# The two transposes that turn an expert's inner layer are issued in the middle of the next expert's first product

## The chip, the cores and the metric

The kernel runs on one core of a Trainium2 chip. The metric is device time in microseconds (us) of one execution. The engines are named as the profile names them: PE is TensorE, DVE VectorE, ACT ScalarE, POOL GpSimd, and SP issues transfers. Every engine works off its own instructions in the order in which they were built.

## The reference, cut to what matters

One layer of a hybrid decoder is computed for 512 prompt and 8 sample tokens (520 rows of 1024): a projection, dilated attention, a state space branch, a merge, a layer norm, and then a mixture of experts with 64 experts, of which each token takes 8. All of it is float32. The part that the change touches is the body of the experts' loop:

```
xb = x_pad[tok]                                   # rows of one expert
h  = jax.nn.silu(xb @ w1[e]) * (xb @ w3[e])       # 1024 -> 256
yb = (h @ w2[e]).astype(jnp.float32)              # 256 -> 1024
return acc.at[tok].add(yb * g[:, None])
```

A shared expert, a gated side input and a second layer norm are added to the result.

## The kernel before, in words

The experts are taken in an order of falling load, and the place of an expert in it is its rank, 0 to 63. A rank has a fixed capacity of 112 down to 56 rows. Float32 products are made as three products of float32r halves: an operand is split into `hi` (a rounded copy, by ScalarE) and `lo` (what is left, by VectorE, or by GpSimd for one item of six), and hi·hi, hi·lo and lo·hi are accumulated (`split`, L267 to L270).

The weights of a rank are six items of 128x1024: four for the first product (w1 and w3 side by side) and two for the second (w2). Each is loaded into one of seven buffers `raw` (L318), split into one of five pairs `hi`, `lo`, and used. `stream.get` (L339) asks for the split of two items beyond the one that it returns.

For rank e the steps are these. `turn` (L1416) transposes the gathered rows, `a<-ident,xg`, in two halves of four transposes, and splits each half into `xgh` and `xgl`. `expert_in` (L1427) makes the first product, `a<-hi,xgh` and so on: four items of six matmuls, 24 in all, into one bank of PSUM, and `ffn_mid` (L1252) makes of it `hg`, by a Silu on ScalarE (L1254) and a product on VectorE. `ffn_turn` (L1258) turns `hg` with two transposes, `a<-ident,hg`, into another bank, and splits that into `hh` (ScalarE) and `hl` (VectorE). `expert_out` (L1435) makes the second product, `mm<-hi,hh` and so on, two items of six matmuls; ScalarE scales it into `y` and GpSimd adds its rows into DRAM by an indirect transfer (L1449). All tiles `a` come from a pool of three banks.

The loop (L1597) issues in iteration e the first product of rank e, the turning of the rows of rank e+1, the second product of rank e-1, and then the turning of `hg` of rank e. So between two first products stand a second product and transposes. Side work (the shared expert, the side input: `x<-ph,...`) is spread over the iterations. The code's order isn't the engines' order: a scheduler places the instructions of each engine by priority and by its own model of time, and takes buffers and banks as it goes. All matmuls have line L210 and all transposes L215, since they go through a helper.

Of the kernel before, what the change touches and what calls it, by code (L numbers as in the profile page):

```python
# [11 lines left out]
def _quiet(*args, **kwargs):  # L12
# [19 lines left out]
NE = 64  # L32
FIXED = 2
CAPS = ([112] * 3 + [100] * 1 + [94] * 1 + [92] * 1 + [88] * 2 + [86] * 1 + [84] * 3 + [82] * 2 + [78] * 7 + [76] * 2 + [74] * 4
        + [72] * 5 + [70] * 4 + [68] * 4 + [66] * 5 + [64] * 7 + [62] * 3 + [60] * 2 + [58] * 2 + [56] * 5)
# [165 lines left out]
def trunk_step(ctx: ExitStack, tc: tile.TileContext, I, O):  # L201
# [3 lines left out]
    class Tensor:  # L205
# [3 lines left out]
        def matmul(self, *a, **k):  # L209
            ins = nc.tensor.matmul(*a, **k)  # L210
            if self.pinned:
                tc.keep_in_program_order(ins)

        def transpose(self, *a, **k):
            ins = nc.tensor.transpose(*a, **k)  # L215
            if self.pinned:
                tc.keep_in_program_order(ins)

    T = Tensor()
# [11 lines left out]
    def open_pool(*a, **k):  # L231
        cm = pool(*a, **k)
        p = cm.__enter__()
        opened.append((p, cm))
        return p

    def close_pool(p):
        at = next(n for n, (q, _) in enumerate(opened) if q is p)
        opened.pop(at)[1].__exit__(None, None, None)
# [15 lines left out]
    def bank():  # L255
        return psa.tile([128, 512], F32, tag="a", name="a")
# [10 lines left out]
    def split(hi, lo, src, e=V):  # L267

        a = S.activation(hi, src, AF.Copy)  # L269
        return a, sub(e, lo, src, hi.bitcast(F32))  # L270
# [974 lines left out]
    def ffn_in(out, xth, xtl, hi, lo, q, rows):  # L1245

        for k in range(2):
            kk = 2 * q + k
            for n, (l, w) in enumerate(((xth, hi), (xth, lo), (xtl, hi))):
                T.matmul(out, lhsT=l[:, kk, rows], rhs=w[:, k], start=(kk == 0 and n == 0), stop=(kk == 7 and n == 2))  # L1250

    def ffn_mid(ps, m):  # L1252
        hg = moe.tile([MAX_CAP, 256], F32, tag="hg", bufs=2, name="hg")
        S.activation(hg[0:m], ps[0:m, 0:256], AF.Silu)  # L1254
        mul(V, hg[0:m], hg[0:m], ps[0:m, 256:512])
        return hg

    def ffn_turn(hg, m):  # L1258
        ps = bank()
        for k in range(2):  # L1260
            T.transpose(ps[:, m * k:m * k + m], hg[0:m, 128 * k:128 * k + 128], ident[0:m, 0:m])
        hh, hl = (moe.tile([128, 2, MAX_CAP], F32R, tag=nm, bufs=2, name=nm)[:, :, 0:m] for nm in ("hh", "hl"))
        H['turned'] = split(hh, hl, ps[:, 0:2 * m].rearrange("p (k t) -> p k t", k=2))
        return hh, hl
# [9 lines left out]
    def shared_mid(out, hg):  # L1274
        S.activation(hg, out[:, 0:128], AF.Silu)
        mul(V, hg, hg, out[:, 128:256])
        return hg

    def shared_turn(hg, i, c):

        ps = bank()
        T.transpose(ps[:, 0:TT], hg, ident[0:TT, 0:TT])
        split(H['shared'][:, i, 0, c], H['shared'][:, i, 1, c], ps[:, 0:TT])
# [12 lines left out]
    def shared_more(i):  # L1296

        if i < 0:
            side_weights(lambda a, b: wd[50 + a // 1024], 2048)
            H['ph'], H['pl'] = (H[k][:, 0:2048].rearrange("p (k n) -> p k n", k=8) for k in ('ph', 'pl'))  # L1300
            return
        out = psx.tile([128, 512], F32, tag="x", name="x")[0:TT, 0:256]
        whole(shared_product(out, i, H['ph'], H['pl'], range(8)))
        shared_turn(shared_mid(out, moe.tile([MAX_CAP, 256], F32, tag="hg", bufs=2, name="sg")[0:TT, 0:128]), i, 1)
# [67 lines left out]
    def second_sums(i):  # L1372

        G.dma_start(H['x1'][:, i], sumsD[1][TT * i:TT * i + TT], accum_op=ALU.add)


    XG, XT, HG, HT, GC, IX = {}, {}, {}, {}, {}, {}
# [28 lines left out]
    def fetch(e):  # L1406
        find(e)
        gather(e)
# [7 lines left out]
    def turn(e):  # L1416
        x, m = XG[e % 3], CAPS[e]
        XT[e] = [moe.tile([128, 8, MAX_CAP], F32R, tag=nm, bufs=2, name=nm)[:, :, 0:m] for nm in ("xgh", "xgl")]
        for z in range(2):
            ps = bank()  # L1420
            for j in range(4):
                k = 4 * z + j
                T.transpose(ps[:, m * j:m * j + m], x[0:m, 128 * k:128 * k + 128], ident[0:m, 0:m])
            src = ps[:, 0:4 * m].rearrange("p (k t) -> p k t", k=4)
            split(XT[e][0][:, 4 * z:4 * z + 4], XT[e][1][:, 4 * z:4 * z + 4], src)

    def expert_in(e):  # L1427
        ps, m = bank(), CAPS[e]
        for q in range(4):
            hi, lo = (t.rearrange("p (k n) -> p k n", k=2) for t in stream.get(AT[e] + q))  # L1430
            ffn_in(ps[0:m], *XT[e], hi, lo, q, slice(0, m))
        HG[e] = ffn_mid(ps, m)
        XT.pop(e)

    def expert_out(e):  # L1435
        ps, m = mm2(), CAPS[e]
        hh, hl = HT.pop(e)
        for k in range(2):
            hi, lo = stream.get(BT[e] + k)
            for n, (l, w) in enumerate(((hh, hi), (hh, lo), (hl, hi))):  # L1440
                for h in range(2):
                    T.matmul(ps[0:m, h], lhsT=l[:, k], rhs=w[:, 512 * h:512 * h + 512], start=(k == 0 and n == 0),
                             stop=(k == 1 and n == 2))
        if e >= NE - 2:
            kept(e, ps)
            return
        y = py.tile([MAX_CAP, 1024], F32, tag="y", bufs=YB, name="y")[0:m]
        S.activation(y.rearrange("p (h n) -> p h n", h=2), ps[0:m], AF.Copy, scale=GC.pop(e)[0:m])  # L1448
        G.indirect_dma_start(out=sumsD[e % 2 if e < SECOND else 0][:, :], out_offset=bass.IndirectOffsetOnAxis(ap=IX.pop(e)[0:m, 0:1], axis=0),  # L1449
                             in_=y, in_offset=None, compute_op=ALU.add)  # L1450
# [24 lines left out]
    def second_phase():  # L1475
# [109 lines left out]
        for e in range(3):  # L1585
            fill(F[1])
            find(e, (1,))
        T.pinned = False
        expert_in(0)
        turn(1)  # L1590
        HT[0] = ffn_turn(HG.pop(0), CAPS[0])
# [5 lines left out]
        for e in range(NE + 1):  # L1597
            if e == NE - 1:
                last_rows()
            if 0 < e < NE:  # L1600
                expert_in(e)
            if 0 < e < NE - 1:
                turn(e + 1)
            if e:
                expert_out(e - 1)
            else:
                H['shared'] = py.tile([128, 5, 2, 2, TT], F32R, tag="side", name="st")
                mids = py.tile([MAX_CAP, 1024], F32, tag="y", bufs=YB, name="mids")
                mids = [shared_mid(H['first half'][i], mids[0:TT, 128 * i:128 * i + 128]) for i in R5]
            if 0 < e < 6:  # L1610
                shared_turn(mids[e - 1], e - 1, 0)
            if 0 < e < NE - 1:
                HT[e] = ffn_turn(HG.pop(e), CAPS[e])
            if e + 3 < NE:
                fetch(e + 3)
            for i in {SECOND + 2: (0, 1, 2), SECOND + 3: (3, 4)}.get(e, ()):
                second_sums(i)
            if e == 4:
                close_pool(pre)
                pw = open_pool("pw")  # L1620
            while side and (e - 4) * SIDE >= N_SIDE - len(side) + 1:
                q, i = side.pop(0)
                if q == -2:
                    shared_more(i)
                elif q == -1:
                    shared_out(i)
                elif q < 4:
                    layer_inputs(q, i)
                else:
                    last_scales(i)  # L1630
# [66 lines left out]
    def last_rows():  # L1697

        yy = pw.tile([128, 2, 1024], F32R, tag="pl", name="yy")
        H['yh'], H['yl'] = yy[:, 0], yy[:, 1]  # L1700
        to = H['to'] = pw.tile([128, 5, TT], F32R, tag="praw", name="to")
        G.memset(yy.bitcast(F32), 0.0)
        G.memset(to.bitcast(F32), 0.0)
        for e in (NE - 2, NE - 1):
            m, z = CAPS[e], 64 * (NE - 1 - e)
            oh = OH.pop(e)
            for tiles in ((0, 1, 2), (3, 4)):
                ps = mm2()[:, 0]
                for n, i in enumerate(tiles):
                    T.matmul(ps[z:z + m, TT * n:TT * n + TT], lhsT=oh[:, i], rhs=ident_b[0:TT, 0:TT], start=True, stop=True)  # L1710
                a, b = tiles[0], tiles[-1] + 1
                S.activation(to[z:z + m, a:b], ps[z:z + m, 0:TT * len(tiles)].rearrange("p (i t) -> p i t", t=TT), AF.Copy)
# [116 lines left out]
    close_pool(gpool)  # L1829
    close_pool(qkv)  # L1830
    second_phase()


# [16 lines left out]
```

## Time and profile before

| | us |
|---|---|
| three runs | 1322.67, 1334.91, 1335.15 |
| their median | 1334.91 |
| the profiled execution | 1326.8 |
| its span, first to last instruction | 1325.1 |

The experts take the span from about 450 to 1290 us. The profile names for each idle time of an engine the instruction that ended it. A row of the timeline gives start, length, instruction, and in brackets the idle time before it with what ended it. Matmuls overlap, so the distance of two starts is the time that one costs.

### The profile page before, as it was taken

What the parts mean: (1) busy time and instruction counts of PE and PEld (TensorE: products, weight loads), DVE (VectorE), ACT (ScalarE), POOL (GpSimd) and SP (SyncE); (2) the same over time, 40 slices, a digit from 0 to 9 for tenths busy, and PEclk for the clock granted to TensorE, in tenths of its full rate; (3) what the DMA queues carried; (4) which work ended last, traced back from release to release, by engine and by line L of the source; (5) the groups of instructions that cost most, each with busy time, mean ns of one, the idle gap of its engine ahead of it and who ended that gap; (6) DMA issues with size and microseconds to landing.
All of it is one profiled execution on the core that took longest, in us unless ns stands there. A gap on an engine that the chain in (4) does not pass through costs nothing. (4 is left out here: it accounts for less than half of the span.)

```text
span 1325.1 us, 20407 instructions
## 1 busy us (share of the span) xinstructions
PE 1188.6 (90%) x7083; PEld 887.7 (67%) x7084; DVE 939.5 (71%) x1397; ACT 700.4 (53%) x1055; POOL 535.2 (40%) x327
## 2 busy tenths in 40 slices
PE   7699999999998979888899888899999999988683
PEld 7699799899877856556566566667666666644341
DVE  7974657833468778576779566788877887766566
ACT  4131535222213566566567556677767776766462
POOL 1822141011124446343656335454554544455325
PEclk9897899999997989888999889999999999989897
DMA  8476563253343699889989978999999999979973
GB/s 295 124 255 114 188 202 121 83 143 96 112 149 103 196 266 252 255 264 294 310 253 322 299 232 280 286 335 318 332 319 309 335 318 293 291 254 279 256 218 93
DMA packets 114236, 312.93 MB, mean 236 GB/s; under 512 B 37041, under 2 KB 37465, under 8 KB 113055
## 3 DMA queue, kind: packets, MB, share of 16 engines
q1 hardware_dynamic: 68307, 247.11, 54.8%
q0 software_dynamic: 30848, 43.33, 15.0%
q10 hardware_dynamic: 14974, 21.14, 6.0%
q8 instruction: 57, 0.93, 0.3%
q14 instruction: 50, 0.41, 0.1%
HBM read 276.32 MB, written 32.87 MB: 233 GB/s over the span
## 5 line engine op out<-in xcount | busy, mean ns | idle before, releaser
L265 DVE TENSOR_TENSOR lo<-raw,hi 128x1024 fp32r<-128x1024 f32 x371 | 519.1, 1410 | 197.9 <-ACT hi L269 193.2
L269 ACT ACTIVATE hi<-raw 128x1024 fp32r<-128x1024 f32 x434 | 450.4, 1055 | 259.6 <-DMA raw<-in_we_dram 107.2
L1449 POOL DMA_INDIRECT accD<-y,idx x62 | 127.4, 2054 | 283.0 <-ACT hh L269 146.9
L210 PE MATMUL a<-hi,xgh 128*64 128x512 f32 (+18 forms) x512 | 212.7, 415 | 7.0 <-ACT hi L269 4.8
L210 PE MATMUL a<-lo,xgh 128*64 128x512 f32 (+18 forms) x512 | 210.8, 412 | 5.2 <-DVE lo L265 5.0
L210 PE MATMUL a<-hi,xgl 128*64 128x512 f32 (+18 forms) x512 | 207.6, 405 | 0.0
L265 POOL TENSOR_TENSOR lo<-raw,hi 128x1024 fp32r<-128x1024 f32 x63 | 169.7, 2694 | 54.2 <-ACT hi L269 45.2
L1412 POOL DMA_INDIRECT xg<-xD,idx x64 | 114.1, 1783 | 104.6 <-DVE idx L1394 43.2
L210 PE MATMUL mm<-xh,hi 128*128 128x260 f32 (+1 forms) x576 | 120.5, 290 | 18.9 <-DVE r L259 10.5
L210 PE MATMUL mm<-xl,hi 128*128 128x260 f32 (+1 forms) x576 | 119.1, 288 | 0.7 <-DVE xl L265 0.7
L210 PE MATMUL mm<-xh,lo 128*128 128x260 f32 (+1 forms) x576 | 119.1, 288 | 0.0
L210 PEld LDWEIGHTS a<-hi,xgh 128*64 128x64 f32 (+18 forms) x512 | 75.9, 148 | 51.8 <-ACT hi L269 8.5
L210 PEld LDWEIGHTS a<-lo,xgh 128*64 128x64 f32 (+18 forms) x512 | 76.1, 149 | 45.2 <-DVE lo L265 10.4
L210 PEld LDWEIGHTS mm<-xh,hi 128*128 128x128 f32 x576 | 91.3, 193 | 19.8 <-issue 10.8
L210 PEld LDWEIGHTS a<-hi,xgl 128*64 128x64 f32 (+18 forms) x512 | 75.6, 148 | 38.4 <-issue 4.5
L210 PE MATMUL mm<-lo,hh 128*64 128x512 f32 (+18 forms) x256 | 86.2, 419 | 15.1 <-POOL lo L265 12.5
L210 PEld LDWEIGHTS mm<-xl,hi 128*128 128x128 f32 x576 | 91.0, 193 | 1.3 <-DVE xl L265 1.0
L210 PE MATMUL mm<-hi,hh 128*64 128x512 f32 (+18 forms) x256 | 85.5, 416 | 7.1 <-ACT hi L269 6.7
L210 PEld LDWEIGHTS mm<-xh,lo 128*128 128x128 f32 x576 | 91.2, 193 | 0.1
L1448 ACT ACTIVATE y<-mm,both 78x1024 f32<-78x1024 f32 (+19 forms) x62 | 68.7, 1107 | 36.1 <-PE mm L210 33.0
L210 PE MATMUL mm<-hi,hl 128*64 128x512 f32 (+18 forms) x256 | 83.6, 409 | 0.0
L215 PEld LDWEIGHTS a<-ident,xg 64*128 64x128 f32 (+18 forms) x512 | 50.9, 146 | 43.1 <-issue 16.8
(410 smaller groups left out, 1971.4 us busy)
## 6 DMA issues: line engine op xcount, KB each, us to landing
raw<-in_we_dram SPq DMA_DIRECT2D x384, 512.0 KB
raw<-in_wd_dram SPq DMA_DIRECT2D x50, 512.0 KB
accD<-zeros_b POOLq DMA_DIRECT2D x2, 2560.0 KB
praw<-in_wp_dram SPq DMA_DIRECT2D x8, 512.0 KB
base<-in_xtok_dram ACTq DMA_DIRECT2D x1, 2080.0 KB
xD<-base ACTq DMA_DIRECT2D x5, 416.0 KB
base<-accD POOLq DMA_DIRECT2D x5, 416.0 KB
acc<-accD SPq DMA_DIRECT2D x5, 416.0 KB
```

Source lines behind the costliest of these rows:

```text
L210: ins = nc.tensor.matmul(*a, **k)
L215: ins = nc.tensor.transpose(*a, **k)
L265: return e.tensor_tensor(out=o, in0=a, in1=b, op=ALU.subtract)
L269: a = S.activation(hi, src, AF.Copy)
L1412: G.indirect_dma_start(out=XG[e % 3][0:m], out_offset=None, in_=xD[:, :], in_offset=bass.IndirectOffsetOnAxis(ap=IX[e][0:m, 0:1], axis=0), ...
L1448: S.activation(y.rearrange("p (h n) -> p h n", h=2), ps[0:m], AF.Copy, scale=GC.pop(e)[0:m])
L1449: G.indirect_dma_start(out=sumsD[e % 2 if e < SECOND else 0][:, :], out_offset=bass.IndirectOffsetOnAxis(ap=IX.pop(e)[0:m, 0:1], axis=0), ...
```

## The change

The turning of `hg` of rank e-1 is taken out of the loop's end and put into `expert_in` of rank e, behind the second of the four items, for ranks 2 to 63. Its two transposes carry an edge that keeps them behind the last matmul of that item on TensorE. The helper returns the instruction for that. Nothing is added or removed: the same transposes, splits and transfers are issued. From here on the helper's transposes have line L216 in the changed kernel and `split` L268 to L271.

```
             ins = nc.tensor.matmul(*a, **k)
             if self.pinned:
                 tc.keep_in_program_order(ins)
+            return ins
...
-                T.matmul(out, lhsT=l[:, kk, rows], rhs=w[:, k], start=(kk == 0 and n == 0), stop=(kk == 7 and n == 2))
+                ins = T.matmul(out, lhsT=l[:, kk, rows], rhs=w[:, k], start=(kk == 0 and n == 0), stop=(kk == 7 and n == 2))
+        return ins
...
         for q in range(4):
             hi, lo = (t.rearrange("p (k n) -> p k n", k=2) for t in stream.get(AT[e] + q))
-            ffn_in(ps[0:m], *XT[e], hi, lo, q, slice(0, m))
+            ins = ffn_in(ps[0:m], *XT[e], hi, lo, q, slice(0, m))
+            if q == 1 and e > 1:
+                with tc.issue_after(ins.ins):
+                    HT[e - 1] = ffn_turn(HG.pop(e - 1), CAPS[e - 1])
         HG[e] = ffn_mid(ps, m)
...
-            if 0 < e < NE - 1:
-                HT[e] = ffn_turn(HG.pop(e), CAPS[e])
```

The scheduler then places much else anew. Three places show it, with the numbers of the buffers in the names.

TensorE where `hg` of rank 28 (`hg_8375`) is turned, before. `a_8479` is the first product of rank 29, whose four items are 8395, 8407, 8480 and 8492.

```order
L210 MATMUL x_8708<-what_3592,oh_8706 70x6
L215 MATMUL a_8422<-ident_69,hg_8375 128x72 x2
L210 MATMUL a_8479<-hi_8395,xgh_8378 72x512
L210 MATMUL a_8479<-lo_8396,xgh_8378 72x512
L210 MATMUL a_8479<-hi_8395,xgl_8379 72x512
```

The same in the changed kernel, where the first product of rank 29 is `a_8472` and its items are 8395, 8407, 8473 and 8485.

```order
L210 MATMUL a_8472<-hi_8395,xgl_8379 72x512
L210 MATMUL a_8472<-hi_8407,xgh_8378 72x512
L210 MATMUL a_8472<-lo_8408,xgh_8378 72x512
L210 MATMUL a_8472<-hi_8407,xgl_8379 72x512
L210 MATMUL a_8472<-hi_8407,xgh_8378 72x512
L210 MATMUL a_8472<-lo_8408,xgh_8378 72x512
L210 MATMUL a_8472<-hi_8407,xgl_8379 72x512
L216 MATMUL a_8497<-ident_69,hg_8375 128x72 x2
L210 MATMUL a_8472<-hi_8473,xgh_8378 72x512
```

The transposes have moved from ahead of the first item's matmuls to behind those of the second.

ScalarE from one `hg` to the next `hh`, before: `hg_8375` is the inner layer of rank 28, `hh_8425` its turned half, and the items 8504 and 8516 are the second product's.

```order
L269 ACTIVATE hi_8348<-raw_8184 128x1024
L269 ACTIVATE hi_8360<-raw_8196 128x1024
L269 ACTIVATE xgh_8378<-a_8380 128x4x72
L269 ACTIVATE hi_8395<-raw_8211 128x1024
L269 ACTIVATE hi_8407<-raw_8243 128x1024
L1254 ACTIVATE hg_8375<-a_8323 72x256
L269 ACTIVATE xgh_8378<-a_8387 128x4x72
L269 ACTIVATE hi_8480<-raw_8255 128x1024
L1448 ACTIVATE y_8419<-mm_8394,both_7848 72x1024
L269 ACTIVATE hi_8492<-raw_8328 128x1024
L269 ACTIVATE hh_8425<-a_8422 128x2x72
```

The same in the changed kernel, where the turned half is `hh_8500`, and 8551 is the first item of rank 30.

```order
L270 ACTIVATE hi_8407<-raw_8243 128x1024
L270 ACTIVATE xgh_8378<-a_8380 128x4x72
L1356 ACTIVATE pt_8312<-x_8281 104x256
L1256 ACTIVATE hg_8375<-a_8316 72x256
L270 ACTIVATE hi_8473<-raw_8255 128x1024
L270 ACTIVATE xgh_8378<-a_8387 128x4x72
L270 ACTIVATE hi_8485<-raw_8321 128x1024
L1453 ACTIVATE y_8419<-mm_8394,both_7841 72x1024
L270 ACTIVATE hi_8504<-raw_8333 128x1024
L270 ACTIVATE hi_8516<-raw_8352 128x1024
L270 ACTIVATE hi_8551<-raw_8367 128x1024
L270 ACTIVATE hh_8500<-a_8497 128x2x72
```

`hg` of rank 28 stands behind the same split in both, that of rank 29's second item. `hh` stood behind the split of rank 29's fourth item, and now stands behind three more, up to rank 30's first item.

TensorE at the end of rank 29's first product, before: `hh_8425` is used, and `a_8543` is the second half of the turning of rank 30's rows.

```order
L210 MATMUL a_8479<-hi_8492,xgh_8378 72x512
L210 MATMUL a_8479<-lo_8493,xgh_8378 72x512
L210 MATMUL a_8479<-hi_8492,xgl_8379 72x512
L210 MATMUL mm_8550<-hi_8504,hh_8425 72x512 x2
L215 MATMUL a_8543<-ident_69,xg0_4185 128x72 x4
```

The same in the changed kernel.

```order
L210 MATMUL a_8472<-hi_8485,xgh_8378 72x512
L210 MATMUL a_8472<-lo_8486,xgh_8378 72x512
L210 MATMUL a_8472<-hi_8485,xgl_8379 72x512
L216 MATMUL a_8543<-ident_69,xg0_4185 128x72 x4
L210 MATMUL mm_8550<-hi_8504,hh_8500 72x512 x2
L210 MATMUL mm_8550<-lo_8505,hh_8500 72x512 x2
L210 MATMUL mm_8550<-hi_8504,hl_8501 72x512 x2
```

The second product still follows the first one, and so stands 12 matmuls of the first product behind the turning of `hg` in place of 24.

## Rows read from the trace of the kernel before

**Rows 1.** The page: the span; busy us, share and instructions of each engine.

```profile
span 1325.1 us, 20407 instructions
PE 1188.6 (90%) x7083; PEld 887.7 (67%) x7084; DVE 939.5 (71%) x1397; ACT 700.4 (53%) x1055; POOL 535.2 (40%) x327
```

**Rows 2.** Stretches: busy us of PE to POOL; granted clock, DMA share, GB/s.

```profile
600.00:650.00 50.00, 43.17 (x231) 29.47 (x230) 39.26 (x51) 35.35 (x51) 20.64 (x11) 0.93 0.92 301
1050.00:1100.00 50.00, 50.00 (x286) 31.94 (x285) 42.27 (x62) 35.51 (x50) 26.61 (x15) 1.00 1.00 326
```

**Rows 3.** Waits of TensorE, 560 to 1290 us: total us, times, longest.

```profile
PE a L215 <- DVE hg L259: 21.9, 12, 3.8
PE mm L210 <- POOL lo L265: 11.8, 10, 2.9
```

**Rows 4.** Tile hg: ns min/median/max; last, idle it ended, us, times.

```profile
L1254 ACT ACTIVATE hg<-a x64: 361/379/386, 455.6 to 1284.9; 78x256 f32<-78x256 f32 x7, 64x256 f32<-64x256 f32 x7, 72x256 f32<-72x256 f32 x5, 66x256 f32<-66x256 f32 x5
L259 DVE TENSOR_TENSOR hg<-hg,a x64: 399/407/418, 456.4 to 1285.3; 78x256 f32<-78x256 f32 x7, 64x256 f32<-64x256 f32 x7, 72x256 f32<-72x256 f32 x5, 66x256 f32<-66x256 f32 x5
...
  PE a L215: 23.5, 14
```

**Rows 5.** TensorE in time, rank 28: start us, length us, instruction [idle before <-releaser].

```profile
847.63 0.34 PE L215 MATMUL a<-ident,hg 72*128 72x72 f32 x2 [3.33 <-DVE hg L259]
...
848.04 0.39 PE L210 MATMUL a<-lo,xgh 128*72 128x512 f32 x1
848.27 0.40 PE L210 MATMUL a<-hi,xgl 128*72 128x512 f32 x1
...
848.90 0.63 PE L210 MATMUL a<-lo,xgh 128*72 128x512 f32 x1
849.32 0.63 PE L210 MATMUL a<-hi,xgl 128*72 128x512 f32 x1
```

**Rows 6.** The same stretch on ScalarE, then VectorE.

```profile
844.93 1.06 ACT L269 ACTIVATE hi<-raw 128x1024 fp32r<-128x1024 f32 x1 [3.09 <-DMA raw<-in_we_dram]
845.89 0.36 ACT L1254 ACTIVATE hg<-a 72x256 f32<-72x256 f32 x1
...
846.02 1.23 DVE L265 TENSOR_TENSOR lo<-raw,hi 128x1024 fp32r<-128x1024 f32 x1 [1.65 <-ACT hi L269]
847.16 0.41 DVE L259 TENSOR_TENSOR hg<-hg,a 72x256 f32<-72x256 f32 x1
```

**Rows 7.** TensorE, then ScalarE, where rank 26 is turned.

```profile
820.43 0.35 PE L215 MATMUL a<-ident,hg 74*128 74x74 f32 x2 [3.30 <-DVE hg L259]
...
817.73 1.06 ACT L269 ACTIVATE hi<-raw 128x1024 fp32r<-128x1024 f32 x1 [3.06 <-DMA raw<-in_we_dram]
```

**Rows 8.** TensorE where ranks 8 and 11 are turned.

```profile
569.12 0.55 PE L215 MATMUL a<-ident,hg 86*128 86x86 f32 x2 [3.27 <-DVE hg L259]
...
610.87 0.54 PE L215 MATMUL a<-ident,hg 84*128 84x84 f32 x2 [3.82 <-DVE hg L259]
```

**Rows 9.** Stretches of 10 us, TensorE: busy, granted clock, DMA share, GB/s.

```profile
610.00:620.00 10.00, 9.13 (x40) 0.68 0.77 226
840.00:850.00 10.00, 6.67 (x39) 0.93 0.91 293
850.00:860.00 10.00, 9.78 (x56) 0.90 0.88 259
```

**Rows 10.** TensorE where rank 60 is turned.

```profile
1238.88 0.46 PE L215 MATMUL a<-ident,hg 56*128 56x56 f32 x2 [3.32 <-DVE hg L259]
...
1243.71 1.10 PE L210 MATMUL mm<-lo,hh 128*56 128x512 f32 x2 [2.91 <-POOL lo L265]
```

**Rows 11.** Waits of ScalarE, 560 to 1290 us.

```profile
ACT hi L269 <- DMA raw<-in_we_dram: 96.8, 73, 3.1
```

**Rows 12.** Tile hh: what writes it and hl, ns min/median/max.

```profile
L269 ACT ACTIVATE hh<-a x64: 244/278/362, 458.7 to 1287.5; 128x156 fp32r<-128x156 f32 x7, 128x128 fp32r<-128x128 f32 x7, 128x144 fp32r<-128x144 f32 x5, 128x132 fp32r<-128x132 f32 x5
L265 DVE TENSOR_TENSOR hl<-a,hh x64: 257/300/380, 459.6 to 1288.6; 128x156 fp32r<-128x156 f32 x7, 128x128 fp32r<-128x128 f32 x7, 128x144 fp32r<-128x144 f32 x5, 128x132 fp32r<-128x132 f32 x5
```

## The prediction

> **What bounds the kernel now.** I read the page first, then stretches of the experts' stage, then who waits for whom on TensorE, and then the timeline of the longest of those waits on three engines. TensorE is busy for 90% of the span [rows 1], and the stage has two faces [rows 2]: from 1050 to 1100 us it is busy without a gap at the full clock with the transfers at a share of 1.00, while from 600 to 650 us it is busy for 43.2 of 50 us, at a granted clock of 0.93, and the transfers run at 301 GB/s where the other stretch has 326. So TensorE sets the pace, and where it has gaps, there is some room in the transfers too.
>
> The largest cause of gaps is the one that the change is about: the transposes of `hg` wait for VectorE, 21.9 us in 12 waits, about twice the next cause [rows 3]; over the whole kernel it is 23.5 us in 14 waits [rows 4]. Five of the 14 are long: 3.27 and 3.82 us at ranks 8 and 11 [rows 8], 3.30 at rank 26 [rows 7], 3.33 at rank 28 [rows 5] and 3.32 at rank 60 [rows 10], 17.0 us together, so the other nine make 6.5.
>
> The reader should now see that making `hg` takes little: 0.38 us on ScalarE and 0.41 on VectorE [rows 4]. What is long is a queue. At rank 28 ScalarE stands for 3.09 us in front of a weight split, because the item hasn't landed; the Silu that makes `hg` is behind that split on ScalarE, and the product that ends it is behind the `lo` half of the same item (1.23 us) on VectorE [rows 6]. Only then do the transposes run, at 847.63. Rank 26 shows the same with 3.06 us [rows 7]. So these waits are a late transfer that reaches TensorE by way of `hg`. What the change is worth hangs on whether TensorE has other work that doesn't need the late item.
>
> **What the change removes.** The transposes now come behind two items (12 matmuls) of the next product. A matmul costs 0.23 us at full clock (848.04 to 848.27 [rows 5]), so `hg` gets 12 x 0.23 = 2.8 us more, and an item is 6 x 0.23 = 1.4 us. By the built order, in the kernel before the split that stands right ahead of `hg` on ScalarE is the next product's second item at ranks 11 and 28, and its first item at ranks 8 and 26.
> At ranks 11 and 28 the first item is ready, so TensorE works 1.4 us of it off during the wait, and the pair of transposes (0.34 us [rows 5]) goes out of the way: 1.8 us gained each, 3.6 together. Then it stands in front of the late item itself.
> At ranks 8 and 26 the late item is the very one that TensorE wants next, with its `lo`. Only the product of `hg` (0.41) and a handover are saved, 0.5 us each, 1.0 together. At rank 60 a wait of 2.91 us for another `lo` follows [rows 10], so nothing is gained.
> Of the nine short waits I take half, 3.2 us, since the trace doesn't say for each which item is next; the bounds are 0 and 6.5.
>
> A stall also costs the clock. After the wait at rank 28 matmuls go from 0.23 to 0.42 us apart (848.90 to 849.32 [rows 5]), which is the lower level, 1.2 of 2.4 GHz. The granted clock is 0.68 over the 10 us after rank 11's stall, and 0.93 and 0.90 around rank 28's [rows 9]: 3.2 and 0.7 + 1.0 us of full-speed work lost. With stalls half as long I take half of 4.9, 2.5 us; the bounds are 0 and 4.9.
> Gained: 3.6 + 1.0 + 3.2 + 2.5 = 10.3 us, between 0 and 23.5 + 4.9 = 28.4.
>
> **What the change adds.** No instruction is added, but three slacks become short.
> First, `hh` and `hl`. The second product that needs them stood 24 matmuls behind the transposes, 5.5 us, and stands 12 behind them now, 2.8 us. And by the built order `hh` now stands on ScalarE behind the split of the item two beyond the second product's first (46 of 63 ranks), where it stood mostly behind items that TensorE needs before it. That split can begin only when the buffer of the next product's second item is free, so about when the transposes run. It takes 1.06 us [rows 6], `hh` 0.28 and `hl` 0.30 [rows 12], the `lo` between them 1.23: `hh` is there some 1.5 us behind the transposes and `hl` some 3, where they are needed at 2.8 and, four matmuls on, at 3.7. The cover is the 12 matmuls, and the margin about 1 us, if the item has landed. ScalarE waited for an item 73 times between 560 and 1290 us, 96.8 us, at most 3.1 [rows 11], so 1.3 us on average. One split in six stands ahead of `hh`: 12 such events, of which I let half exceed the margin by 1 us: 6 us, and 2 for the clock.
> Second, banks. In the built kernels the first product gets the bank of the product before it at 33 of 61 ranks, before at 16. There its first matmul, not the transposes, waits for `hg`, and the wait comes back where it was: I charge 2 us, of bounds 0 and 10.
> Third, the second half of the turning of rows always takes the bank of the turned `hg` (61 of 61, before 56) and so waits for `hl`, and the split rows are used sooner. It runs within a microsecond or two of the second product's start, so the first term holds most of it; 1 us more.
> Added: 6 + 2 + 2 + 1 = 11 us.
>
> Everything else is as before: side work moves from inside the first products to between them, but is the same; splits, gathers and scatters are the same in number on ScalarE, VectorE, GpSimd and SP, and shift with TensorE.
>
> Sum: -10.3 + 11 = +0.7 on the profiled execution's 1326.8 us, 1327.5. That execution lies 8 us below the median of the runs shown and 4 above the lowest of them, so I forecast **1328 us**, and count 1322 to 1348 us (the median within 1%) as no change, about what a measurement of this kernel can tell.
>
> **The rivals.**
> *The waits end and nothing takes their place.* For it: five stalls of over 3 us, each with a slow stretch behind, and transfers that have 8% of room where the stalls are [rows 2]. Against it: a late item stands behind each of the long ones that I followed. All of the 28.4 us gives 1298; with two thirds of it, 1308.
> *The stall moves to the second product* and grows. The place is ScalarE in front of `hh`: TensorE may not begin the second product until an item two beyond is split, so where transfers set the pace, it must keep two items in hand where one or none was enough. It decides once that split is more than 1 us late at more than one rank in four. At half of the 52 ranks from 560 to 1290 us with 1 us each, and 2 us of slow clock at one in six, it costs 26 + 17 = 43, less the 10 gained: 1360. At a quarter it costs 13 + 8 - 10 = 11: 1338. I take 1347. For it: the 73 late items [rows 11]. Against it: these 73 made only 12 waits of the transposes so far [rows 3].
> *The bank.* With the same bank in turn, Silu and product of a first product lie bare ahead of the next: 0.38 + 0.41, 0.9 us with handovers, at 17 more ranks, 15 us, so 1342. Against it: a second product of 12 matmuls, 2.8 us, stands between the two, and before, too, 16 ranks had one bank in turn.
> The Trainium skill asks for what this rival is about: in Perfetto Trace Analysis, section Matmuls, independent groups should rotate through the banks, so that ScalarE and VectorE empty one while the next group runs. By that rule alone this change would be slower; no run here shows it yet.
> That the change isn't made can be left out: the built order has the transposes behind the second item.
>
> **How the numbers follow.** My forecast has a chance of 0.50, the vanishing wait 0.25, the moved stall 0.20, the bank 0.05. Faster by over 1% is the vanishing wait, 0.25; slower is the moved stall and half of the bank, 0.22; within 1% is the rest, 0.53. The range goes from 1306, which leaves out the far half of the first rival, to 1346, which leaves out the far half of the second. The forecast's own range is 1316 to 1340.
>
> **What would show it.** In the changed profile, waits of the transposes of `hg` for VectorE should fall from 23.5 to below 5 us. What replaces them should be named: first matmuls of an item waiting for `hi` or `lo` right after a stall of ScalarE for a transfer (the late item itself), second products waiting for `hh` or `hl`, or turned rows waiting for `hl`, some 6 us, and first products waiting for `hg`, some 2. If those sums stay under 5 us and the granted clock from 600 to 650 us rises from 0.93 towards 1.00, the first rival holds. If second products wait for `hh` for over 20 us, the second does. My prediction would be wrong at its root if the items landed at other times altogether because TensorE's pace is new.

## The result and the profile after

The changed kernel takes 1347.76 us (median of six runs, 1339.29 to 1354.99), the kernel before 1332.97 in the six runs beside it: the ratio is 1.0115, with an interval of 1.0084 to 1.0146. It is slower by 1.15%, some 15 us. The forecast was 1328, and the time lies 2 us above the range of 1306 to 1346.

The profiled execution of the changed kernel is its fastest one, 1339.29 us; its span is 12.4 us longer than that of before [rows 1]. First the page, then two stretches, with the columns of [rows 2].

```profile
span 1337.5 us, 20420 instructions
PE 1189.0 (89%) x7082; PEld 887.3 (66%) x7084; DVE 969.3 (72%) x1397; ACT 707.5 (53%) x1055; POOL 537.7 (40%) x327
```

```profile
600.00:650.00 50.00, 42.77 (x254) 29.96 (x252) 34.80 (x51) 34.18 (x50) 22.54 (x11) 1.00 0.96 305
1050.00:1100.00 50.00, 49.19 (x274) 30.84 (x273) 42.23 (x56) 37.78 (x51) 23.41 (x13) 1.00 0.97 314
```

TensorE's busy time is the same, so all of the loss is in gaps, the times in which TensorE stands idle. From 600 to 650 us the clock rose from 0.93 to 1.00 and the gaps stayed. What the gaps are is in the waits of TensorE, 450 to 1290 us (total us, times, longest), of the changed kernel, the largest five, and behind them one line of the kernel before.

```profile
PE a L216 <- DMA xg<-xD,idx: 27.9, 5, 7.6
PE a L216 <- DVE hl L266: 12.4, 17, 2.1
PE mm L210 <- ACT hh L270: 9.7, 8, 2.4
PE mm L210 <- POOL lo L266: 7.9, 7, 1.8
PE a L216 <- DVE sg L260: 6.9, 5, 2.5
```

```profile
PE a L215 <- DMA xg<-xD,idx: 15.8, 3, 7.9
```

The waits for `hg`, 23.5 us [rows 4], are gone but for one of 0.7. Two things stand in their place: the short cover (`hh` for second products, `hl` for turned rows that take the same bank), 22.1 us, and rows that the gathers bring too late, 27.9 us in place of 15.8. The second was in no step of the prediction. The groups of instructions on the page (busy us, mean ns, idle us before them and what ended most of it) show on which side of the gather the delay arises, first before, then after.

```profile
L1412 POOL DMA_INDIRECT xg<-xD,idx x64 | 114.1, 1783 | 104.6 <-DVE idx L1394 43.2
```

```profile
L1414 POOL DMA_INDIRECT xg<-xD,idx x64 | 126.3, 1974 | 197.7 <-DVE idx L1396 154.7
```

GpSimd sits idle for the row numbers `idx`, 43.2 us before and 154.7 after. `idx` is what the search `x<-what,oh` on TensorE finds, so the searches come later. Rank 23 shows it. Here are TensorE and GpSimd of the changed kernel (start, length, instruction, idle before).

```profile
740.05 0.32 PE L210 MATMUL x<-what,oh 104*74 104x6 bf16 x5
...
762.44 1.22 PE L216 MATMUL a<-ident,xg 74*128 74x74 f32 x8 [7.41 <-DMA xg<-xD,idx]
...
767.23 0.63 PE L210 MATMUL a<-lo,xgh 128*74 128x512 f32 x1
767.66 0.63 PE L210 MATMUL a<-hi,xgl 128*74 128x512 f32 x1
```

```profile
743.09 2.01 POOL L1414 DMA_INDIRECT xg<-xD,idx  x1 [3.63 <-DVE idx L1396]
```

And the same rank in the kernel before.

```profile
708.16 0.32 PE L210 MATMUL x<-what,oh 104*74 104x6 bf16 x5
...
744.98 1.19 PE L215 MATMUL a<-ident,xg 74*128 74x74 f32 x8
```

```profile
712.82 2.20 POOL L1412 DMA_INDIRECT xg<-xD,idx  x1 [0.18 <-PE x L210]
```

Before, the gather is issued 32 us ahead of the turning that needs its rows; after, at 743.09, and the rows are used 19.4 us later. TensorE loses 7.41 us and then works for a while at the lower level of its clock (0.43 us from matmul to matmul, a granted clock of 0.61 over the 10 us from 762.4). Over ranks 3 to 63, a turning begins 25.0 us (median) behind the end of its gather's issue before, and 19.3 after. Why: by the order on TensorE, the search stands some 27 us of TensorE work ahead of the turning before and 20 after (matmuls of 512 columns counted at 0.23 us, of 256 at 0.12, others at 0.05; medians). Searches and side work take turns in the one `x` bank in the order of the code, and the scheduler now places most of them between the first products: of the 305 matmuls of the searches, 130 stand inside a first product before and 53 after.

ScalarE waits for weight items for 68.6 us, less than the 96.8 of [rows 11].

```profile
ACT hi L270 <- DMA raw<-in_we_dram: 68.6, 44, 3.6
```

### The profile page after: what moved, and what is told of

It reads as the page before. It is cut to its first block, busy times and chain, and to the rows that moved or that the text cites. A ratio compares the mean times of both kernels' runs of the same rounds, so it can differ in the third digit from the quotient of the medians.

```text
span 1337.5 us, 20420 instructions
## 1 busy us (share of the span) xinstructions
PE 1189.0 (89%) x7082; PEld 887.3 (66%) x7084; DVE 969.3 (72%) x1397; ACT 707.5 (53%) x1055; POOL 537.7 (40%) x327
## 5 line engine op out<-in xcount | busy, mean ns | idle before, releaser
L266 DVE TENSOR_TENSOR lo<-raw,hi 128x1024 fp32r<-128x1024 f32 x371 | 546.5, 1483 | 167.3 <-ACT hi L270 166.1
L1454 POOL DMA_INDIRECT accD<-y,idx x62 | 120.8, 1948 | 224.7 <-ACT y L1453 168.6
L1414 POOL DMA_INDIRECT xg<-xD,idx x64 | 126.3, 1974 | 197.7 <-DVE idx L1396 154.7
L266 POOL TENSOR_TENSOR lo<-raw,hi 128x1024 fp32r<-128x1024 f32 x63 | 186.1, 2954 | 36.1 <-ACT hi L270 31.4
L210 PEld LDWEIGHTS mm<-xh,hi 128*128 128x128 f32 x576 | 91.7, 194 | 22.6 <-issue 13.8
L216 PEld LDWEIGHTS a<-ident,xg 64*128 64x128 f32 (+18 forms) x512 | 50.6, 147 | 83.4 <-issue 34.6
L216 PE MATMUL a<-ident,xg 64*128 64x64 f32 (+18 forms) x512 | 63.0, 245 | 46.3 <-DMA xg<-xD,idx 27.9
L210 PE MATMUL mm<-hi,hl 128*64 128x512 f32 (+18 forms) x256 | 87.5, 425 | 0.0
```

What stands on the lines that cost most here:

```text
L266: return e.tensor_tensor(out=o, in0=a, in1=b, op=ALU.subtract)
L1414: G.indirect_dma_start(out=XG[e % 3][0:m], out_offset=None, in_=xD[:, :], in_offset=bass.IndirectOffsetOnAxis(ap=IX[e][0:m, 0:1], axis=0), ...
```

## The experiments

Theory A: the short cover of `hh` and `hl` is the loss (the prediction's second rival). Theory B: the loss is the place that the scheduler gives to searches, gathers and side work. Ratios are to the kernel before, beside it on the same chip.

**hhfirst**

```
+            if q == 3 and e > 1:
+                a, b = H['turned']
+                with tc.issue_after(a.ins), tc.issue_after(b.ins):
+                    stream.split_to(AT[e] + 6)
```

> The change, and one thing more: the splits of the items that lie beyond the second product's first one are kept behind hh on ScalarE and behind hl on VectorE. In the built order hh then stands behind the split of the second product's first item (60 of 63 ranks) and no longer behind two more; the token search of the gathers stays where the change put it (23.1 us of TensorE work ahead of the turning, changed kernel 21.5, before 27.3). Theory A (the short cover of hh and hl is what costs): waits of the second product for hh fall from 10.1 to under 4 us, those of turned rows for hl from 12.4 to about 6, and the time falls from 1348 to about 1336. Theory B (the gathers are issued late, and the gathered rows with them): gather waits stay at 15 to 30 us and the time stays at 1343 or more.

1.0182 (1.0136 to 1.0227), 1355.6 us. Theory A missed: no second product waits for `hh` any more, waits for `hl` are down from 12.4 to 0.8 us, and the loss grew. B's bounds are met (21.6 us of gather waits), but B doesn't say why the time is 8 us above the changed kernel's. ScalarE now stands in front of `hh` until the transposes have run, 7.8 us in the change and 96.1 here, and its other work stands behind it (560 to 1290 us; total, times, longest).

```profile
ACT hh L270 <- PE a L216: 96.1, 42, 5.1
```

So the new place of `hh`, behind three more splits, which the prediction counted as a cost, was the better of the two.

**fetch, q2, b_late**

```
 fetch:   fetch(e + 3) written behind expert_in(e)
 q2:      -            if q == 1 and e > 1:
          +            if q == 2 and e > 1:
 b_late (of the kernel before): fetch(e + 3) written behind the side work
```

> The change, and the search and gather of rank e+3 written right behind the first product of rank e, ahead of the turning of rank e+1. In the built order the search stands 28.4 us of TensorE work ahead of the turning that needs its rows (changed kernel 21.5, before 27.3). Turned layer still 12 matmuls ahead of the second product; hh stands behind fewer splits than in the change (at 43 of 63 ranks behind none beyond the second product's first). Theory A: some half of the 22.5 us of waits for hh and hl goes with those splits, 1340 or so, and gather waits are no matter. Theory B: gather waits fall from 27.9 to under 10 us and the late transfers behind them too, 1330 to 1336.

> The change with the turning behind the third item in place of the second: hg gets 18 matmuls, hh only 6 matmuls (1.4 us at full clock, 1.8 us in the built order) ahead of the second product. In the built order the token search stands 32.8 us ahead of the turning that needs its rows, earlier than in either kernel. The two theories go opposite ways. Theory A: hh comes 1.6 to 2.0 us behind the transposes, more than its cover at most ranks, so second products wait for hh 20 to 60 us in all, and the time is 1360 or more. Theory B: gather waits under 10 us, and the time is below the changed kernel's, 1345 or less.

> The kernel before, with the turning where it was, and only the search and gather of rank e+3 written behind the side work in place of ahead of it. In the built order the search stands 17.8 us of TensorE work ahead of the turning that needs its rows (before 27.3, changed kernel 21.5). Theory A: nothing of hh and hl changes, so within 5 us of the kernel before. Theory B: gather waits rise from 15.8 to 30 us or more and the time by at least 10 us, to 1343 or more.

fetch: 1.0063 (1.0031 to 1.0094), 1336.7 us, gather waits down from 27.9 to 0.9 us, and about half of the loss gone, between what A and B asked for. q2: 1.0070 (1.0042 to 1.0098), 1340.3 us, with half the cover of the change and 26 us of waits for `hh` and `hl`, as B asked and against theory A, which asked for 1360. b_late: 1.0101 (1.0066 to 1.0136), the change's loss without the change, as B asked. One line of fetch, two of q2 and one of b_late:

```profile
PE a L216 <- DMA xg<-xD,idx: 0.9, 1, 0.9
```

```profile
PE a L216 <- DVE hl L266: 17.8, 17, 2.9
...
PE mm L210 <- ACT hh L270: 8.4, 6, 2.4
```

```profile
PE a L215 <- DMA xg<-xD,idx: 32.6, 9, 7.1
```

**held_move.** To keep the scheduler out, a table gives each engine's instructions in the order wanted, and a chain of edges that fix the issue order alone holds them there.

```
+        hold(tc, nc)
...
+            if last is not None:
...
+                tc.add_manual_dep(i, last.name, free, reason="the table's order")
+            last = i
```

> The change's move alone. A table at the end of the loop holds every engine to the order of the kernel before; only the two transposes of each hg stand behind the second item of the next first product, the halves of the rows' turning that stood ahead of that place (33 of 122) right behind them, and the scheduler places only hh and hl. Searches, gathers and side work stand where they stood before. Theory A (the short cover of hh and hl costs): hh and hl still stand 12 matmuls ahead, so most of the loss stays, 1340 or more, with 15 us or more of waits for hh and hl. Theory B (what costs is the new place that the scheduler gives to searches, gathers and side work): the loss is gone, 1336 or less, gather waits near the 15.8 us of before. If the move itself pays the 10.3 us that the prediction put on it, below 1325.

1.0180 (1.0130 to 1.0230), 1356 us: against theory B as I had put it, and within the bounds of A. But the move wasn't alone: in an order made for other places, the transposes' users stand wrong. TensorE's second halves of rows wait for `hl` more than twice as long as in the change (27.2 us), and ScalarE stands in front of `hh` for 56.8 us, where it did so for 2.9 before.

```profile
PE a L298 <- DVE hl L348: 27.2, 24, 8.6
```

```profile
ACT hh L352 <- PE a L298: 56.8, 31, 7.8
```

**b_free_hg, a_free_rows, b_free_rows, a_free_layer, a_free_all** keep the order of their kernel by such a table, and take one dependence out (a_free_all takes out two). In their traces every engine works in the order of their own kernel, and no instruction is added. No run holds an order with nothing taken out.

```
 b_free_hg:  transpose(..., hg[0:m, ...], ...)  ->  transpose(..., ident[0:m, 0:128], ...)
 *_rows:     transpose(..., x[0:m, ...], ...)   ->  the same from rank 3 on
 *_layer:    split(hh, hl, H['xh'][:, 0:2, 0:m].bitcast(F32));  lhsT=H['xh' if l is hh else 'xl'][:, k, 0:m]
```

> The kernel before in its own order on every engine, held by a table, with one dependence taken out: the transposes of hg read the constant identity in place of hg, so they never wait for it (hg is still made; the experts' result is wrong). It prices all 23.5 us of the removed waits, with nothing put in their place. By the prediction's sum the half of it that isn't behind a late item is worth 10.3 us, 1321; if the waits only go over to the late items, hi or lo, behind them, less than 4 us, 1327 to 1333, and waits for hi and lo rise by about as much; if all goes, 1303 to 1307.

> The changed kernel in its own order on every engine, held by a table, with one dependence taken out: from rank 3 on the turning of rows reads the constant identity in place of the gathered rows, so that no transpose waits for a gather. Gathers still run. Theory B in its narrow form (late gathers alone are the loss): 28 us of waits and the slow clock behind them go, time 1330 or less. Theory A: 1342 or more, since hh and hl are as they were. If side work in one block and the short cover share the loss, in between.

> The same release in the kernel before, in its own order, held by a table: the control for the release in the changed kernel. 15.8 us of gather waits are there to go. If the two kernels differ by gathers alone, both releases end at the same time within 5 us; if not, the changed kernel stays slower by what the gathers don't explain.

> The changed kernel in its own order on every engine, held by a table, with the turned layer's dependences taken out: hh and hl are made from the halves of the normed input, and the second product reads those halves in place of hh and hl, so that no second product waits for hh or hl, and no turned row for hl (the experts' result is wrong). Gathers are as they were. The release of the rows took 21.0 us off the changed kernel and 12.4 off the kernel before, so 9.8 us of the loss are left for the layer. If they are the short cover of hh and hl (22.5 us of waits), this kernel is 8 to 12 us faster than the changed one, 1336 to 1340. If they are the order of all the rest, under 4 us.

> The changed kernel in its own order, held, with both releases: rows and layer. If gathers and cover are the whole loss, it comes down to the kernel before with its rows released, 1317, to 4 us; if the order of the rest costs too, it stays above 1322.

| | ratio | interval |
|---|---|---|
| b_free_hg | 0.9994 | 0.9972 to 1.0016 |
| b_free_rows | 0.9911 | 0.9880 to 0.9941 |
| a_free_rows | 0.9967 | 0.9946 to 0.9988 |
| a_free_layer | 1.0088 | 1.0056 to 1.0120 |
| a_free_all | 0.9999 | 0.9965 to 1.0033 |

b_free_hg: the transposes' 23.5 us of waits for `hg`, taken out with nothing put in their place, are worth nothing that the interval shows, 4 us at most. What stands there instead is waits for weight items (`hi`, `lo` on either engine), 31.2 us in all before and 46.5 here, and for the side work's `sg`, 3.0 before and 9.2 here. And 5.8 us of waits still end with `hg`: instructions that don't read it wait for the bank that it is made from. These are the longest of each kind.

```profile
PE mm L327 <- POOL lo L382: 15.2, 14, 2.5
PE a L327 <- ACT hi L386: 13.3, 7, 3.8
PE a L327 <- DVE lo L382: 9.7, 17, 1.1
PE a L332 <- DVE sg L376: 9.2, 3, 4.2
...
PE a L327 <- DVE hg L376: 4.4, 4, 2.7
```

Where the transposes had their long waits, TensorE now stands in front of these, at ranks 8, 28 and 60 (start, length, instruction, idle before).

```profile
571.54 0.31 PE L332 MATMUL a<-ident,sg 104*128 104x104 f32 x1 [4.16 <-DVE sg L376]
...
847.11 0.70 PE L327 MATMUL a<-hi,xgh 128*72 128x512 f32 x1 [2.74 <-DVE hg L376]
...
1243.63 0.67 PE L327 MATMUL a<-hi,xgh 128*56 128x512 f32 x1 [3.81 <-ACT hi L386]
```

The rows: without gather waits the changed kernel gains 0.0148 (1.0115 to 0.9967), 20 us, the kernel before 0.0089, 12 us. So late gathers are 8 us of the 15, give or take 6 by the three intervals. The layer: without any wait for `hh` or `hl` the changed kernel gains 0.0027 with its gathers, give or take 0.0045, and nothing without them (0.9967 to 0.9999, give or take 0.0039). So 22 us of waits for the layer cost about nothing, and theory A falls; released of its gathers alone, the changed kernel shows even more of them and is a little faster than the kernel before.

```profile
PE mm L315 <- ACT hh L375: 18.7, 12, 4.6
PE a L321 <- DVE hl L371: 15.6, 20, 1.8
```

**a_mm, b_mm, a_mm_q0**

```
-        ps = bank()
+        if e is None:
+            ps = bank()
+        else:
+            H['mm', e] = mm2()
+            ps = H['mm', e][:, 1]
...
-            for n, (l, w) in enumerate(((hh, hi), (hh, lo), (hl, hi))):
-                for h in range(2):
+            for h in range(2):
+                for n, (l, w) in enumerate(((hh, hi), (hh, lo), (hl, hi))):
```

> The change, with the turned hg written into one half of the second product's own PSUM buffer (two of them, rotating) in place of one of the three banks; the second product is issued half by half, so that the half with the turned hg comes last. In the built order the second half of the rows' turning stands inside the first product again at 49 of 60 ranks (changed kernel 0, before 33), and the search 26 us ahead of its turning (changed kernel 20, before 27). hh and hl still stand 12 matmuls ahead of the second product. Theory D (the middle of a first product is the place where the three banks are short: the product holds one, the turned hg takes the one that the rows' turning needs, and everything behind it moves back): waits of turned rows for hl go from 12.4 to under 2 us, gather waits to 16 or less, time 1336 or less and within 5 us of the same buffer in the kernel before. Theory A (short cover of hh and hl): 10 us or more of waits for hh stay and the time is 1340 or more.

> The control: the same buffer for the turned hg in the kernel before, with the turning where it was (24 matmuls ahead). Both theories: within 1% of the kernel before, 1320 to 1340; theory D: the changed kernel with this buffer is as fast to 5 us; theory A: that one is slower by 10 us or more.

> As the change with the turned hg in the second product's buffer, and the turning behind the first item in place of the second: 18 matmuls of cover for hh in place of 12 (4.9 us in the built order in place of 3.5, control 6.1). Theory A: its time lies between that of the control and that of the change with this buffer, some 4 us under the latter. Theory D: no difference among the three beyond 5 us.

a_mm 1.0103 (1.0070 to 1.0136), a_mm_q0 1.0042 (1.0006 to 1.0077), and the control b_mm 1.0187 (1.0142 to 1.0232). The control, which was to change nothing, is the slowest, so the three say nothing of banks or cover. In it second products wait for the `lo` of GpSimd, 32.5 us where it was 12.5 before.

```profile
PE mm L210 <- POOL lo L265: 32.5, 20, 4.0
```

By then nine kernels with nine placements, the change among them, were slower than before, by 0.4 to 1.9%. That led to the test that decides: another placement, and nothing else.

**one_rank, held_pool**

```
 one_rank (of the kernel before):
-            if 0 < e < NE - 1:
+            if 0 < e < NE - 1 and e != 7:
                 turn(e + 1)
             if e:
                 expert_out(e - 1)
+                if e == 7:
+                    turn(e + 1)
 held_pool: the order of the kernel before, with lo and gather swapped on GpSimd at five ranks
```

> The kernel before, with two statements swapped in one iteration of 64: in iteration 7 the second product is written ahead of the rows' turning. The turning of hg is where it was at every rank. The scheduler answers with another placement from there to the end: 1336 of 6806 matmuls and transposes out of the order of before (the change: 1530), the search 17 us ahead of its turning (before 27, the change 20), the second half of the rows' turning inside the first product at 5 of 60 ranks (before 33, the change 0). Theory A: as the kernel before, to 5 us. Theory B: the placement alone costs about what the change costs, 1343 or more, with gather waits of 25 us or more.

> The kernel before in its own order on every engine, held by a table, but for five places on GpSimd: at ranks 4, 16, 40, 47 and 48 the gather is issued ahead of the lo split that stood right in front of it (2.4 to 3.4 us each). In the profile of before the gathers of ranks 4 and 16 ran 2.6 us after they could have, and their rows were waited for, 7.9 and 4.6 us. If late gathers cost what the release says, 3 to 6 us are gained (ratio 0.996 or so); if the lo split delayed behind them is waited for, nothing.

one_rank: 1.0101 (1.0064 to 1.0138). Two statements swapped in one iteration of 64 cost what the change costs, with the turning of `hg` untouched. A turning of rows begins 15.7 us behind its gather's issue, and gather waits are the longest of all the kernels.

```profile
PE a L215 <- DMA xg<-xD,idx: 39.6, 10, 7.1
PE a L215 <- DVE hg L259: 14.2, 14, 2.7
```

held_pool: 1.0028 (1.0001 to 1.0054), no gain. Gather waits fell from 15.8 to 11.0 us, but second products waited for the `lo` behind the gathers, 20.7 us in place of 12.5.

```profile
PE mm L327 <- POOL lo L382: 20.7, 15, 3.3
PE a L332 <- DVE hg L376: 18.5, 12, 3.7
PE a L332 <- DMA xg<-xD,idx: 11.0, 3, 4.1
```

**from8, after_one_rank**

```
 from8:   -            if q == 1 and e > 1:
          +            if q == 1 and e > 8:
          ...
          +            if 0 < e < 8:
          +                HT[e] = ffn_turn(HG.pop(e), CAPS[e])
 after_one_rank: the swap of one_rank, in iteration 2 of the changed kernel
```

> The change from rank 8 on; up to there the turning of hg stands where the kernel before has it. 54 ranks of 62 have the change, with the same 12 matmuls of cover (3.3 us in the built order). But the scheduler's placement is another one: the search stands 28 us of TensorE work ahead of its turning (changed kernel 20, before 27). If the placement is what the change paid for, not the moved transposes: gather waits under 12 us and a time within 0.7% of the kernel before, 1323 to 1340. If the moved transposes cost it, 54 ranks of 62 have 13 of the 15 us, 1344.

> The change at all ranks, with two statements swapped in iteration 2 alone (the second product written ahead of the rows' turning). The search then stands 25 us ahead of its turning in place of 20, the cover of hh is the same. Placement theory: between the changed kernel and the one before, 1335 to 1344, with gather waits under 20 us. If the moved transposes cost it: 1345 or more.

from8: 1.0012 (0.9991 to 1.0033), with 7.5 us of gather waits. after_one_rank: 0.9982 (0.9957 to 1.0008), 1329.7 us, faster than either theory asked for: the move is there at every rank, and the whole loss is gone. A turning of rows begins 26.0 and 22.9 us behind its gather's issue (changed kernel 19.3). The gather waits of from8, and then the waits of after_one_rank, 450 to 1290 us (of a profiled execution of 1336.45 us):

```profile
PE a L216 <- DMA xg<-xD,idx: 7.5, 1, 7.5
```

```profile
PE mm L210 <- POOL lo L266: 22.7, 17, 3.7
...
PE a L216 <- DMA xg<-xD,idx: 12.0, 3, 8.0
...
PE a L216 <- DVE hl L266: 8.4, 10, 2.9
```

No version that does the whole work beats the kernel before beyond its interval. Of the twelve kernels with another order and nothing taken out (held_pool aside), ten are slower beyond it and two are level. Some of them carry other edits too, but it is a hint that the kernel before has a good placement, which an edit is likelier to lose than to better.

## Why the prediction was wrong

**The failing step** is the sentence that side work and gathers are "the same in number" and "shift with TensorE", costed at nothing. (Of side work it says that it "is the same".) Their number is the same and their place is not: the searches moved 7 us of TensorE work closer to the turnings, and the gathers, which take 15.4 to 17.5 us from the end of their issue to the rows' use at the five waits, came late. The releases put 8 of the 15 us on that, give or take 6. A swap of two statements that costs as much without the move (one_rank), and one that takes the loss away with the move in place (after_one_rank), put the whole of it on the placement. Some 5 of the 20 us between forecast and result are the base of the sum: it started from the profiled execution, 1326.8, where the six runs have 1332.97. The built order showed the place of the searches beforehand, in the same list of TensorE that I read at three places; I followed the transposes and not what the scheduler did with the rest.

**Removed, 10.3 us of 0 to 28.4**: worth about 0, the lower bound (b_free_hg). Something else stands behind nearly every long wait, and seldom what I had there. At rank 60 it is a late item (3.81 us). At ranks 8 and 11 it is the turning of the side work's `sg` (4.16 and 3.58 us), which ScalarE and VectorE make behind a late item's split; the prediction has no such step. At rank 28 it is the bank of `hg` (2.74 us), so TensorE can't work on the first item there, ready or not. At rank 26 no wait is left behind the transposes in that execution. Three terms went wrong with it, the 3.6 us at ranks 11 and 28, half of the short waits, and the clock.

**Added, 11 us of waits and their clock**: the waits came, and larger, 22.1 us for `hh` and `hl` where I had 6 and 1, three times as much. Their price in time was about 0 and not 11 (a_free_layer, a_free_all): taken out, they leave the time as it was, and others grow, in a_free_layer those for `sg` from 6.9 to 13.8 and for `xgl` from 4.4 to 11.5 us. Both halves of my sum counted waits as time, with opposite signs. Their difference, +0.7 us, is about what the move shows by itself where the placement keeps the gathers early (0.9982 and 1.0012), but that is luck, since neither half is worth what I put on it.

**The bank.** No first product of the changed kernel waits for `hg`, though 33 of 61 first products get the bank of the one before; a second product of 12 matmuls stands between, as the prediction had it. By the rule of the Trainium skill (Perfetto Trace Analysis, section Matmuls, independent groups should rotate through the banks) that was a loss; the changed kernel's trace doesn't show one. In b_free_hg, which has the order of the kernel before, it does show such waits: first products wait for `hg` four times, 4.4 us in all.

**The second rival** gave the better time, 1347, by a mechanism that isn't there: it asked for over 20 us of second products waiting for `hh`, there are 9.7, and taking them away gains nothing that the intervals show. **The first** is refuted by b_free_hg. None of the cases had the scheduler's placement as a mechanism of its own.

**What stays open.** With the rows released in both, the changed kernel is still 0.0056 (7.5 us, give or take 5) behind. It is neither the layer (a_free_all) nor the gathers. The swaps show that it belongs to the placement, not which part of that: in a_free_all rows' halves `xgl` and the bank of the searches are waited for, 16.5 and 11.8 us, where other waits stand in b_free_rows.

```profile
PE a L315 <- DVE xgl L371: 16.5, 13, 3.7
...
PE x L315 <- DVE both L1498: 11.8, 6, 3.3
```

That late gathers alone don't order the placements is seen in hhfirst, held_move and b_mm: 19.5 to 21.6 us of gather waits, and the three slowest times.

## What to carry to other kernels

Where a scheduler places the instructions, an edit that moves one step is two changes, the step and a new placement of everything else; measure the second by itself, with an edit elsewhere that means nothing (here a swap at one of 64 ranks) and with the old order held, before the step is judged. Before predicting, read in the built order how far each long transfer's issue stands ahead of its first user, for the transfers that the edit doesn't name too. And price a wait by taking its cause away, not by its length: 23.5 us of waits on the busiest engine were worth nothing that could be measured, 15.8 us of others were worth 12.

## What had not been expected of the hardware

Two kinds of wait on the same engine have very different prices. Removing the transposes' waits for `hg` gave 0.9994 and all waits for `hh` and `hl` 0.0027, both within the intervals, while removing 15.8 us of gather waits, three of 3.4 to 7.9 us, gave 0.9911, 12 us. What tells the two kinds apart stays open. Here are the 10 us behind the three gather waits of the kernel before, at ranks 4, 16 and 56 (columns of [rows 2]).

```profile
492.00:502.00 10.00, 9.61 (x44) 7.36 (x45) 4.87 (x10) 6.42 (x10) 2.15 (x2) 0.75 0.52 157
...
662.00:672.00 10.00, 9.78 (x46) 6.76 (x47) 6.09 (x11) 6.26 (x9) 2.03 (x2) 0.72 0.53 175
```

```profile
1169.70:1179.70 10.00, 10.00 (x33) 4.94 (x34) 4.98 (x7) 4.71 (x8) 1.35 (x1) 0.68 0.91 285
```

And behind two of the five long waits for `hg`, at ranks 8 and 28.

```profile
569.10:579.10 10.00, 8.39 (x38) 5.61 (x39) 7.16 (x11) 6.87 (x12) 4.21 (x3) 0.68 0.77 238
...
847.60:857.60 10.00, 9.97 (x54) 6.83 (x55) 6.53 (x10) 7.88 (x11) 7.26 (x4) 0.83 0.87 266
```

Behind the first two gather waits the transfers run at 157 and 175 GB/s, a share of 0.52 and 0.53; behind all five long waits for `hg` at 224 to 266 GB/s, 0.77 to 0.97. That would make lost transfers the price of a gather wait. But behind the third gather wait they run at 285 GB/s and 0.91, and the clock doesn't tell the two apart: it is 0.68 to 0.75 behind gather waits and 0.55 to 0.83 behind waits for `hg`. So this is a guess from two stretches of three, and no run tested it alone.
